# Norm roots spread by two split products, the sample's attention a step earlier, and a last norm with half the sum products

## The chip, the cores and the metric

The kernel runs on one core of a Trainium2 chip. The core has five engines with a queue of instructions each: TensorE (PE: matrix products and transposes, with its weight loads listed apart as PEld), VectorE (DVE), ScalarE (ACT), GpSimd (POOL) and SyncE (SP, which here only issues transfers). Engines run beside one another and wait for each other on semaphores. The metric is the time of one execution on the device in microseconds, lower is better.

## The reference

One layer of a decoder is computed for a prompt of 512 positions and, separately, for 8 samples of 4 new positions with a cache of 128 earlier keys and values. Everything is float32. Each of the two halves of the layer is wrapped in two RMS norms:

```
def _rmsnorm(x, g):
    y = x32 * lax.rsqrt(jnp.mean(x32 * x32, axis=-1, keepdims=True) + EPS) * g
...
h    = rmsnorm(x, norm_mix_pre)
m    = mixer(h)            # input projection, RG-LRU branch, windowed attention, gates, w_out
x    = x + rmsnorm(m, norm_mix_post)
f    = conv_ffn(rmsnorm(x, norm_ffn_pre))   # w_up, causal conv of width 3, gelu, w_down
x    = x + rmsnorm(f, norm_ffn_post)
```

The model width is 1024, the feed-forward width 4096, with 8 query heads and 2 key heads of 128. The sample's attention works on 128 cached and 4 own keys, with a learned sink and a relative bias.

## The kernel before

**Layout.** Activations stand transposed: 8 tiles of 128 channels by 544 columns, 512 positions of the prompt and 32 of the sample. Most stages work on them in two halves of columns, 256 and 288 (HALF) or 272 and 272 (HALF2).

**Products.** All large products are made of split operands: a value is written as the sum of two fp32r tiles, high (H, made on ACT by a copy into fp32r) and low (L, made on DVE by subtracting the high part), and three products HH, LH and HL are added up in PSUM. `wsplit_hi` (L283) and `wsplit_lo` (L290) do this for the weights as they arrive (`raw_*` to `wh_*`, `wl_*`), `wh_e`, `wl_e` are the same for the weights of the feed-forward (L1485, L168).

**Norms.** The columns of a tile are positions, so the root of a norm (one number for each position) has to be repeated over the 128 channels. This is done on PE: DVE multiplies the identity by the roots, which gives a diagonal (`dg`, three tiles of up to 128 columns), and PE multiplies a tile of ones by that diagonal, in plain F32. The result `rep` has each column's root in every partition. There are seven such spreads: two at the start for the norm of `x` (`roots`, L536 to L560, `ps_rep0` with 256 columns and `ps_rep2` with 288), four in `norm_chain` (L1240 and on: `rep_m` and `rep_f` for either half, 272 columns), and one at the end in `finish_b` (`rep_o`, 288 columns). The roots come from sums of squares: `sq_sum` adds squares of the eight channel tiles into `acc` (squares on ACT, sum on DVE), `stats` (L1157) sums over the partitions by products of `acc` with a column of ones (`pst_*`), and `newton_rstd` (L413) takes the root on ACT and refines it in five small DVE instructions.

**The first spread** is issued inside a product of the input projection: `mids` holds functions that run between the products with the weights' high part and those with the low part.

**Last norm.** Before, the squares of the last channel tile went to a tile of their own (`sq7`), and `stats` took three products on `acc` and three on `sq7`. After it, `finish_b` scales each of the eight tiles `ft` (DVE) and adds the residual `x1r` (POOL), two tiles to a step; rows are then turned by PE transposes (`pyo`), copied and stored. Meanwhile PE makes the last products of the first half as rows of tokens (`ptok`).

**The sample's attention** is the generator `sample_attn` (two groups of four samples): loads of the cached keys and values into buffers of the pool `raw` (five buffers, shared with the weights' loads), transposes of the keys on DVE (`kcT`), scores on PE (`pss`), softmax in two parts (`ss`, `st_smp`; DVE and ACT), transposes of the probabilities on PE (`pst`), copies (`spt`), the product with the values (`pso`). Each `yield` hands over to the next step.

**What sets the order.** PE's queue is written in program order. A step is one product of an input tile by a weight tile; `tick` advances a counter by one, and `start_at(t, gen)` starts a generator at step t, `yield n` continues it n steps later (L190 and on). For the mixer the other engines' order is the program's too. From `stats` on (L1157) ACT, DVE and POOL are ordered by a scheduler that looks at dependencies and priorities, so an added instruction can change its neighbours' places. Each engine then runs its queue in that order. Loads wait for their buffer: `raw_wg` (the gates' weights), `raw_in` and the cache blocks use the same five.

Of the kernel before, what the change touches and what calls it, by code (L numbers as in the profile page):

```python
# [11 lines left out]
F32 = mybir.dt.float32  # L12
F32R = mybir.dt.float32r
AF = mybir.ActivationFunctionType
ALU = mybir.AluOpType
AX = mybir.AxisListType

P = 128
# [17 lines left out]
FLAT = SEQ + 7 * DB  # L36
# [37 lines left out]
SAMPLE = (41, 46)  # L74
# [49 lines left out]
def hawk_step(ctx, tc, I, O):  # L124
    nc = tc.nc
    act, dve, pool, pe = nc.scalar, nc.vector, nc.gpsimd, nc.tensor

    keep = ctx.enter_context(tc.tile_pool(name="const", bufs=1))
# [4 lines left out]
    smp = ctx.enter_context(tc.tile_pool(name="small", bufs=4))  # L133
# [12 lines left out]
    def T(name, dt=F32):  # L146
        return tp.tile([P, FLAT + 4], dt, tag="t", name=name)
# [13 lines left out]
    def f32(ap):  # L161
        return ap.bitcast(F32)

    def mm(out, l, r, start, stop):
        pe.matmul(out, l, r, start=start, stop=stop)  # L165

    def sub(out, a, b):
        dve.tensor_tensor(out=out, in0=a, in1=b, op=ALU.subtract)  # L168
# [14 lines left out]
    def start_at(t, gen):  # L183
        serial[0] += 1
        side.append([t, serial[0], gen])
# [29 lines left out]
            tick()  # L215


    ones = keep.tile([P, P], F32, name="ones")
    pool.memset(ones, 1.0)
    ident = keep.tile([P, P], F32, name="ident")  # L220
    make_identity(nc, ident)
    epst = keep.tile([P, 1], F32, name="epst")
    pool.memset(epst, EPS)


    w_in, w_up, w_dn = I["w_in"][0], I["w_up"][0], I["w_down"][0]
# [307 lines left out]
    ps_ohp = []  # L534

    def roots(i0, i1):  # L536
        dg = T(f"dg_{i0}")
        t0 = TOK[i0][0]
        spans = [(TOK[i][0] - t0, TOK[i][1], i) for i in range(i0, i1)]
        n = spans[-1][0] + spans[-1][1]  # L540
        last.append(lambda: xrstd(i0, i1))
        for o, w, i in spans:
            last.append(lambda o=o, w=w, i=i: dve.tensor_scalar(dg[:, o:o + w], ident[:, :w], ss[:, 1, i:i + 1], None,
                                                                ALU.mult))
        yield

        def spread_roots():
            ps = PX(f"ps_rep{i0}")
            mm(ps[:, 0:n], ones, dg[:, 0:n], True, True)
            if not i0:  # L550
                mm(ps[:NH, 256:256 + WIN], relx, ohp, True, True)
                ps_ohp.append(ps)
            act.copy(rep[:, t0:t0 + n], ps[:, 0:n])

        if i0:
            spread_roots()
        else:
            mids.insert(0, spread_roots)
# [318 lines left out]
    def sample_attn(g):  # L877
        kcT = []
        kb = RAW(f"cache_win_k{g}")
        src = I["cache_win_k"][0, 4 * g:4 * g + 4].rearrange("b (e j) k (a d) -> a k j (b e) d", e=4, a=4)  # L880
        for kv in range(NKV):
            for a in range(4):
                nc.sync.dma_start(out=kb[32 * a:32 * a + 32, 512 * kv:512 * kv + 512].rearrange("p (x d) -> p x d", d=32),
                                  in_=src[a, kv])
        vraw = RAW(f"cache_win_v{g}").rearrange("p (b x) -> p b x", b=4)
        nc.sync.dma_start(out=vraw, in_=I["cache_win_v"][0, 4 * g:4 * g + 4].rearrange("b j k d -> j b (k d)"))
        yield 2
        kb4 = kb.rearrange("p (k b x) -> p k b x", k=NKV, b=4)
        for half in range(2):
            kt = S(f"kcT{g}{half}")  # L890
            dve.transpose(kt[:, 0:512].rearrange("p (b k x) -> p k b x", b=2, k=NKV), kb4[:, :, 2 * half:2 * half + 2, :])
            kcT.append(kt)
        yield
        ps = PX(f"pss{g}")
        qg = qs[:, 4 * g:4 * g + 4, :, :].rearrange("p b h t -> p (b h t)")
        mm(ps[:, 2 * WIN:SKEY], qg, kn.rearrange("p k n -> p (k n)"), True, True)
        for b in range(4):
            mm(ps[32 * b:32 * b + 32, 0:2 * WIN], qs[:, 4 * g + b, :, :].rearrange("p h t -> p (h t)"),
               kcT[b // 2][:, (b % 2) * 256:(b % 2) * 256 + 256], True, True)
        yield  # L900
        s = T(f"ss{g}")
        stt(s[:, 0:SKEY], ps[:, 0:SKEY], SCALE, biasS[:, g, :], ALU.mult, ALU.add)
        s3 = s[:, 0:SKEY].rearrange("p (o j) -> p o j", o=1)
        se = softmax_a(s3, 1, sinkr, f"smp{g}")
        yield
        softmax_b(s3, 1, *se)
        yield
        px = PX(f"pst{g}")
        pe.transpose(px[:, 0:P], s[:, 0:P], ident)
        pe.transpose(px[:, P:2 * P], s[:, P:2 * P], ident)  # L910
        pe.transpose(px[:64, 2 * P:3 * P], s[:, 2 * P:SKEY], ident)
        yield
        pt = T(f"spt{g}")
        dve.tensor_copy(pt[:, 0:2 * P], px[:, 0:2 * P])
        dve.tensor_copy(pt[:64, 2 * P:3 * P], px[:64, 2 * P:3 * P])
        yield
        po = PX(f"pso{g}")
        mm(po[:, 0:HD], pt[:64, 2 * P:3 * P], vnt, True, False)
        for kv in range(NKV):
            for b in range(4):  # L920
                mm(po[32 * b:32 * b + 32, 0:HD], pt[:, kv * P + 32 * b:kv * P + 32 * b + 32],
                   vraw[:, b, kv * HD:(kv + 1) * HD], False, kv == NKV - 1)
        yield
        so = T(f"so{g}")[:, 0:HD]
        dve.tensor_copy(so, po[:, 0:HD])
        yield
        px = PX(f"psot{g}")
        pe.transpose(px[:, 0:P], so, ident)
        yield
        ov = px[:, 0:P].rearrange("p (b h t) -> p b h t", b=4, h=NH)  # L930
        parts_ = [[A.t[hd][z][:, SEQ + 16 * g:SEQ + 16 * g + 16].rearrange("p (b t) -> p b t", b=4) for z in range(2)]
                  for hd in range(NH)]
        for hd, (oh, ol) in enumerate(parts_):
            act.activation(oh, ov[:, :, hd, :], AF.Copy)
        yield
        for hd, (oh, ol) in enumerate(parts_):
            sub(ol, ov[:, :, hd, :], f32(oh))
# [124 lines left out]
    start_at(19, sample_rows())  # L1062
    start_at(SAMPLE[0] - 4, scale_qs())
    for g in range(2):
        start_at(SAMPLE[g] - 3, sample_attn(g))
    for c in range(8):
        start_at(GATES[c], gates(c))
        start_at(EXPS[c], lru_exp(c))
# [85 lines left out]
    mixer.close()  # L1154


    def stats(acc, nch, nm, more=None):  # L1157

        ps = PX("pst_" + nm)
        for z in range(nch):  # L1160
            mm(ps[:, z:z + 1], acc[:, z * P:(z + 1) * P], ones[:, 0:1], z == 0, more is None and z == nch - 1)
        for z in range(nch if more is not None else 0):
            mm(ps[:, z:z + 1], more[:, z * P:(z + 1) * P], ones[:, 0:1], False, z == nch - 1)
        st = SM("nst_" + nm, [P, 3, 4], "nst")
        v, r, s_ = (st[:, z, :nch] for z in range(3))
        newton_rstd(r, v, s_, ps[:, :nch])
        return r

    def diag(r, n, nm):
        dg = T("dg_" + nm)  # L1170
        for z in range((n + P - 1) // P):
            w = min(P, n - z * P)
            dve.tensor_scalar(dg[:, z * P:z * P + w], ident[:, :w], r[:, z:z + 1], None, ALU.mult)
        return dg

    def spread(dg, n, nm):

        rep = PX("rep_" + nm)
        mm(rep[:, :n], ones, dg[:, :n], True, True)
        return rep  # L1180

    def sq_sum(acc, src, n, first, nm):
        if first:
            act.activation(acc[:, :n], src, AF.Square)
            if n % P:
                pool.memset(acc[:, n:n + P - n % P], 0.0)
        else:
            sq = T("sq_" + nm)
            act.activation(sq[:, :n], src, AF.Square)
            add(acc[:, :n], acc[:, :n], sq[:, :n])  # L1190
# [538 lines left out]
    x1r = {}  # L1729
# [73 lines left out]
                start_at(now[0] + 3, ffn_states(g0, g1))  # L1803

    yp, ys = O["y_p"][0], O["y_s"].rearrange("b t d -> (b t) d")
    sq7 = {}

    def finish_b(acc):

        lo, hi = HALF[1]  # L1810
        n = hi - lo
        dg = diag(stats(acc, 3, "o1", sq7), n, "o1")
        yield FB[0]
        rep = spread(dg, n, "o1")
        for c in range(8):
            f_ = ft[c][:, lo:hi]
            stt(f_, f_, pv[:, G_FPOST + c:G_FPOST + c + 1], rep[:, :n], ALU.mult, ALU.mult)
            pool.tensor_tensor(out=f_, in0=f_, in1=x1r[c][:, lo:hi], op=ALU.add)
            if c % 2:
                yield 0.5  # L1820

# [10 lines left out]
                between()  # L1832
        return lambda q=nc.sync: q.dma_start(out=dst, in_=o[:nn, :])

    sq7 = T("sq7")
    frow, fgs = {}, {}

    def last_done(c, acc):
        def f(a, ps):
            lo, hi = HALF[a]  # L1840
            n = hi - lo
            f_ = ft[c][:, lo:hi]
            add(f_, f_, ps[:, :n])
            if c < 7:
                sq_sum(acc, f_, n, c == 0, f"ft{a}_{c}")
            else:
                sq_sum(sq7, f_, n, True, "")
        return f

    def turned(i, kk):  # L1850
# [157 lines left out]
```

## Time and profile before

| | |
|---|---|
| median of 3 runs | 977.51 us (977.38 to 977.61) |
| the profiled execution | 977.74 us |
| its span | 976.0 us |
| granted TensorE clock, mean | 0.998 |
| DMA | 147 GB/s mean, 143.07 MB |

A row of the timeline has the start and the length in microseconds, the engine, the line of the program, the operation, output and inputs by the program's names, and where the engine idled before it, for how long and whom it waited for. Rows of the same kind that follow each other directly are put together ("x3"), with the time from the first start to the last end. A matrix product's length is the time from its start until its result is out; products overlap, so what a product costs is read from the distance between starts. An F32 product shows as two records. A row of the list of waits names the waiting and the releasing instruction, then the total wait, how often, and the longest.

### The profile page before, as it was taken

The page shows a single profiled execution, that of the slowest core. Times are in us where ns is not written, and L with a number is a line of the kernel's source. Part 1 is how long each engine was busy: PE and PEld are TensorE (multiplying, and loading weights), DVE is VectorE, ACT ScalarE, POOL GpSimd, SP SyncE. Part 2 cuts the span into 40 slices and gives each one's busy share as a digit, 9 for nine tenths or more (in the row PEclk, how much of TensorE's full clock was granted, in tenths as well). Part 3 has the DMA queues.
Part 4 walks back from the last instruction along what each step waited for, and adds up shares of the span by engine and source line. Part 5 has one row for each costly group of instructions (what it writes and reads, how often), then busy time and mean ns, then how long its engine had stood idle before and what let it go on. Part 6 is the DMA issues. An engine that isn't in the chain of part 4 may idle for free.

```text
span 976.0 us, 20122 instructions
## 1 busy us (share of the span) xinstructions
PE 967.6 (99%) x7668; PEld 959.9 (98%) x7668; DVE 758.6 (78%) x1632; ACT 551.0 (56%) x1344; POOL 168.8 (17%) x288
## 2 busy tenths in 40 slices
PE   9999999999999999999999999999999999999997
PEld 8999999999999999999999999999999999999996
DVE  5777888857858555699967888787888888888875
ACT  6544443467476435556767665655555555556652
POOL 2152000003306331230011111101011101011024
PEclk9999999999999999999999999999999999999999
DMA  7875535632334547136157585858586766768612
GB/s 217 237 239 163 151 88 147 161 93 87 109 113 126 175 121 189 45 122 184 39 114 189 126 191 129 184 137 177 140 179 157 169 156 160 166 140 221 201 30 92
DMA packets 234204, 143.07 MB, mean 147 GB/s; under 512 B 25012, under 2 KB 218940, under 8 KB 234076
## 3 DMA queue, kind: packets, MB, share of 16 engines
q1 hardware_dynamic: 224300, 120.21, 43.9%
q0 software_dynamic: 9696, 19.42, 11.9%
q10 hardware_dynamic: 112, 2.17, 0.6%
q8 instruction: 60, 0.98, 0.4%
q14 instruction: 36, 0.29, 0.1%
HBM read 115.59 MB, written 15.17 MB: 134 GB/s over the span
## 4 chain that ended last, share of the span: by engine, by line
PE 97%; DVE 1%; ACT 1%; DMA 0%; issue 0%; SPq 0%; POOL 0%; ACTq 0%; POOLq 0%
PE pmin L165 20%; PE pmdn L165 19%; PE pux L1536 16%; PE puy L1536 8%; PE pq L1536 7%; PE pmout L165 5%; PE pmlo L165 5%; PE pmao L165 5%; PE puz L1536 4%; PE pg L165 1%; PE pvp L165 1%; PE psc L165 1%; PE ptok L165 1%; DMA pt<-pd 0%; PE ps_warm L165 0%; PE pm_first L165 0%
## 5 line engine op out<-in xcount | busy, mean ns | idle before, releaser
L165 PE MATMUL pmin<-hH,wh_in 128*128 128x256 f32 (+1 forms) x568 | 164.0, 291 | 0.0
L165 PE MATMUL pmin<-hL,wh_in 128*128 128x256 f32 (+1 forms) x568 | 162.5, 288 | 0.0
L165 PE MATMUL pmin<-hH,wl_in 128*128 128x256 f32 (+1 forms) x568 | 159.3, 288 | 0.0
L165 PE MATMUL pmdn<-fH,wh_dn 128*128 128x256 f32 (+1 forms) x448 | 129.3, 289 | 0.0
L165 PE MATMUL pmdn<-fH,wl_dn 128*128 128x256 f32 (+1 forms) x448 | 129.2, 288 | 0.0
L165 PE MATMUL pmdn<-fL,wh_dn 128*128 128x256 f32 (+1 forms) x448 | 129.0, 288 | 0.0
L165 PEld LDWEIGHTS pmin<-hH,wh_in 128*128 128x128 f32 x568 | 107.3, 189 | 1.2 <-issue 1.0
L165 PEld LDWEIGHTS pmin<-hL,wh_in 128*128 128x128 f32 x568 | 107.4, 189 | 0.1
L165 PEld LDWEIGHTS pmin<-hH,wl_in 128*128 128x128 f32 x568 | 104.8, 188 | 0.2 <-issue 0.2
L177 DVE SCALAR_TENSOR_TENSOR uc<-u,fv,uc 128x560 f32<-128x560 f32 x128 | 102.0, 797 | 1.7 <-ACT uc L1567 1.1
L165 PEld LDWEIGHTS pmdn<-fL,wh_dn 128*128 128x128 f32 x448 | 84.4, 188 | 0.0
L165 PEld LDWEIGHTS pmdn<-fH,wl_dn 128*128 128x128 f32 x448 | 84.4, 188 | 0.0
L165 PEld LDWEIGHTS pmdn<-fH,wh_dn 128*128 128x128 f32 x448 | 84.4, 188 | 0.0
L1664 ACT COPY u<-pux 128x272 f32<-128x272 f32 x52 | 20.1, 386 | 84.4 <-PE pux L1536 84.2
L168 DVE TENSOR_TENSOR u<-puy,u 128x240 f32<-128x240 f32 (+2 forms) x78 | 24.6, 343 | 48.8 <-PE puy L1536 32.2
L174 DVE TENSOR_TENSOR ft<-ft,pmdn 128x256 f32<-128x256 f32 (+1 forms) x104 | 45.0, 434 | 15.7 <-PE pmdn L165 15.7
L283 ACT ACTIVATE wh_in<-raw_in 128x512 fp32r<-128x512 f32 x70 | 42.2, 625 | 20.7 <-issue 11.0
L290 DVE TENSOR_TENSOR wl_in<-raw_in,wh_in 128x512 fp32r<-128x512 f32 x70 | 47.8, 694 | 1.0 <-ACT wh_in L283 1.0
L1567 ACT ACTIVATE uc<-u,fv 128x560 f32<-128x560 f32 x64 | 48.2, 755 | 0.0
L779 ACT ACTIVATE s<-s,st 128x256 f32<-128x256 f32 (+1 forms) x32 | 15.2, 475 | 53.8 <-DVE st L776 46.1
L168 DVE TENSOR_TENSOR wl_dn<-raw_dn,wh_dn 128x512 fp32r<-128x512 f32 x56 | 38.3, 685 | 3.8 <-ACT wh_dn L1485 3.8
L1474 POOL DMA_DIRECT2D raw_up_s<-raw_up_s x26 | 22.4, 861 | 95.8 <-DMA raw_up_s<-raw_up__11277 5.4
(761 smaller groups left out, 3388.5 us busy)
## 6 DMA issues: line engine op xcount, KB each, us to landing
raw_in<-in_w_in_dram SPq DMA_DIRECT2D x35, 512.0 KB
raw_dn<-in_w_down_dram SPq DMA_DIRECT2D x56, 256.0 KB
raw_up_s<-in_w_up_dram SPq DMA_DIRECT2D x25, 512.0 KB
raw_up_s<-raw_up_s POOLq DMA_DIRECT2D x26, 256.0 KB, 5.3
raw_ao<-in_w_attn_o_dram SPq DMA_DIRECT2D x8, 512.0 KB
raw_lo<-in_w_lru_o_dram SPq DMA_DIRECT2D x8, 512.0 KB
raw_out<-in_w_out_dram SPq DMA_DIRECT2D x8, 512.0 KB
pd<-pb SPq DMA_DIRECT2D x12, 256.0 KB
```

Source lines behind the costliest of these rows:

```text
L165: pe.matmul(out, l, r, start=start, stop=stop)
L168: dve.tensor_tensor(out=out, in0=a, in1=b, op=ALU.subtract)
L174: dve.tensor_tensor(out=out, in0=a, in1=b, op=ALU.add)
L177: dve.scalar_tensor_tensor(out=out, in0=a, scalar=s_, in1=b, op0=op0, op1=op1)
L283: act.activation(hl[0], raw, AF.Copy)
L290: (eng or dve).tensor_tensor(out=hl[1], in0=raw, in1=f32(hl[0]), op=ALU.subtract)
L779: act.activation(s3[:, j, :], s3[:, j, :], AF.Exp, bias=ng[:, j:j + 1], accum_out=sm[:, j:j + 1])
L1474: pool.dma_start(out=w["p4"], in_=w["p2"], accum_op=ALU.add)
L1536: pe.matmul(ps[:, :HN], w, x, start=start and k == 0 and i == 0, stop=stop and k == 3 and i == 2, skip_group_check=True)
L1567: act.activation(yt[j][:, 0:FLATU], u[:, 0:FLATU], AF.Copy, scale=fv[:, j:j + 1])
L1664: act.copy(e[nm_], z)
```

## The change

Five things change.

1. `ones` becomes an fp32r tile (read as F32 by `stats`). A new `diag` rounds the roots to fp32r (`rh`, a DVE CAST), takes the remainder (`rl`, a DVE subtraction), and makes two diagonals: of `rh` on DVE as before, of `rl` on ACT. `spread_to` then adds two fp32r products in place of one F32 product. All seven spreads use it.
2. `sample_attn` starts one step earlier, and a step is added between its softmax and the transposes, so that the transposes stay where they were and all before them is a step earlier.
3. In the last norm the eighth tile's squares are added into `acc` like the others, and `stats` takes three products.
4. In `finish_b` the residual of odd tiles is added on DVE, that of even tiles on POOL.
5. By these the order of some transfers moves too: the second group's cache block is now loaded ahead of the gates' weights `raw_wg`, in the buffer that `raw_wg` had, and `raw_wg` takes the cache block's later.

```diff
+    onesr = keep.tile([P, P], F32R, name="ones")
+    ones = f32(onesr)
...
+    def diag(r, n, nm):
+        nch = (n + P - 1) // P
+        rs = smp.tile([P, 2, 4], F32R, tag="rs", name="rs_" + nm)
+        rh, rl = (rs[:, z, :nch] for z in range(2))
+        dve.tensor_copy(rh, r)
+        sub(rl, r, f32(rh))
+        wide = 2 * n > FLAT
+        t_ = [T(f"dg{x}_{nm}", F32R) for x in ("hl" if wide else "b")]
+        dh, dl = t_[0][:, 0:n], (t_[1][:, 0:n] if wide else t_[0][:, n:2 * n])
+        for z in range(nch):
+            c = slice(z * P, min(n, z * P + P))
+            w = c.stop - c.start
+            dve.tensor_scalar(dh[:, c], ident[:, :w], f32(rh[:, z:z + 1]), None, ALU.mult)
+            act.activation(dl[:, c], ident[:, :w], AF.Copy, scale=f32(rl[:, z:z + 1]))
+        return dh, dl
+
+    def spread_to(ps, dg):
+        for z in range(2):
+            mm(ps, onesr, dg[z], z == 0, z == 1)
...
-        for o, w, i in spans:
-            last.append(lambda o=o, w=w, i=i: dve.tensor_scalar(dg[:, o:o + w], ident[:, :w], ss[:, 1, i:i + 1], None,
-                                                                ALU.mult))
+        last.append(lambda: dg.extend(diag(ss[:, 1, i0:i1], n, str(i0))))
...
-            mm(ps[:, 0:n], ones, dg[:, 0:n], True, True)
+            spread_to(ps[:, 0:n], dg)
...
         softmax_b(s3, 1, *se)
-        yield
+        yield 2
...
-        start_at(SAMPLE[g] - 3, sample_attn(g))
+        start_at(SAMPLE[g] - 4, sample_attn(g))
...
-        mm(rep[:, :n], ones, dg[:, :n], True, True)
+        spread_to(rep[:, :n], dg)
...
-        dg = diag(stats(acc, 3, "o1", sq7), n, "o1")
+        dg = diag(stats(acc, 3, "o1"), n, "o1")
...
-            pool.tensor_tensor(out=f_, in0=f_, in1=x1r[c][:, lo:hi], op=ALU.add)
+            (dve if c % 2 else pool).tensor_tensor(out=f_, in0=f_, in1=x1r[c][:, lo:hi], op=ALU.add)
...
-            if c < 7:
-                sq_sum(acc, f_, n, c == 0, f"ft{a}_{c}")
-            else:
-                sq_sum(sq7, f_, n, True, "")
+            sq_sum(acc, f_, n, c == 0, f"ft{a}_{c}")
```

How this moves instructions is shown at three places. A row has the line, the operation, and output and inputs.

ACT at the first spread, before: `ss` is the root of the first two blocks of positions, `wh0_in_8` and `wh1_in_8` the high parts of a weight tile that PE needs next, `rep` the copy of the spread roots.

```order
L435 ACTIVATE jk0_1_313,ss_169<-x0_1_107 128x512
L418 ACTIVATE ss_169<-ss_169,epst_95 128x2
L283 ACTIVATE wh0_in_8_353<-raw_in_8_114 128x512
L283 ACTIVATE wh1_in_8_356<-raw_in_8_114 128x512
L553 COPY rep_257<-ps_rep0_378 128x256
```

The same stretch of ACT's queue now:

```order
L457 ACTIVATE jk0_1_313,ss_169<-x0_1_107 128x512
L440 ACTIVATE ss_169<-ss_169,epst_95 128x2
L240 ACTIVATE dgb_0_328<-ident_90,rs_0_325 128x128 x2
L305 ACTIVATE wh0_in_8_358<-raw_in_8_114 128x512
L305 ACTIVATE wh1_in_8_361<-raw_in_8_114 128x512
L572 COPY rep_257<-ps_rep0_383 128x256
```

The two low diagonals, which read the remainder `rs_0`, now stand between the root and the copies of the weights.

DVE at the spread `rep_m` of the first half, before: `nst_m0` are the roots, `dg_m0` their diagonals, `wl_e` the low part of a weight tile whose high part ACT makes.

```order
L177 SCALAR_TENSOR_TENSOR nst_m0_5641<-nst_m0_5641 128x3 x2
L1173 TENSOR_SCALAR dg_m0_5661<-ident_90,nst_m0_5641 128x128 x2
L1173 TENSOR_SCALAR dg_m0_5661<-ident_90,nst_m0_5641 128x16
L168 TENSOR_TENSOR wl_e_0_1_5877<-raw_up_0__5781,wh_e_0_1_5876 128x512
L177 SCALAR_TENSOR_TENSOR mt0_5289<-mt0_5289,pv_141,rep_m0_5681 128x272
```

And the same place of DVE's queue now, with `rs_m0` for the rounded roots and their remainder:

```order
L177 SCALAR_TENSOR_TENSOR nst_m0_5655<-nst_m0_5655 128x3 x2
L231 CAST rs_m0_5675<-nst_m0_5655 128x3
L168 TENSOR_TENSOR wl_e_0_1_5904<-raw_up_0__5802,wh_e_0_1_5903 128x512
L168 TENSOR_TENSOR rs_m0_5675<-nst_m0_5655,rs_m0_5675 128x3
L239 TENSOR_SCALAR dgb_m0_5678<-ident_90,rs_m0_5675 128x128 x2
L239 TENSOR_SCALAR dgb_m0_5678<-ident_90,rs_m0_5675 128x16
L177 SCALAR_TENSOR_TENSOR mt0_5303<-mt0_5303,pv_141,rep_m0_5701 128x272
```

The weight's low part now stands between the rounding and the remainder, ahead of the diagonals. At the other three spreads of `norm_chain` the CAST, the remainder and the diagonals stand together where the diagonals were.

DVE in the second group of the sample's attention, before: `s3_3` is a softmax of the prompt, `wl1_in_5` a weight's low part, `spt0` the copies of the first group's turned probabilities, `kcT10` and `kcT11` the second group's turned keys.

```order
L787 TENSOR_SCALAR s3_3_2623<-s3_3_2623,st_3_3_2625 128x256 x2
L290 TENSOR_TENSOR wl1_in_5_2674<-raw_in_5_2378,wh1_in_5_2673 128x512
L171 TENSOR_TENSOR xr4_2676<-pmin_4_1_2648,rep_257 128x256
L171 TENSOR_TENSOR xr4_2676<-pmin_4_1_2648,rep_257 128x8x4
L168 TENSOR_TENSOR tL3_1_2732<-pt3_1_2556,tH3_1_2731 128x512
L821 STREAM_TRANSPOSE pb3_3_2735<-s3_3_2623 128x512
L914 COPY spt0_2739<-pst0_2692 128x256
L915 COPY spt0_2739<-pst0_2692 64x128
L891 STREAM_TRANSPOSE kcT10_2742<-cache_win_k1_2636 128x2x2x128
L891 STREAM_TRANSPOSE kcT11_2744<-cache_win_k1_2636 128x2x2x128
```

The same stretch now:

```order
L806 TENSOR_SCALAR s3_3_2651<-s3_3_2651,st_3_3_2653 128x256 x2
L910 STREAM_TRANSPOSE kcT10_2710<-cache_win_k1_2598 128x2x2x128
L910 STREAM_TRANSPOSE kcT11_2712<-cache_win_k1_2598 128x2x2x128
L312 TENSOR_TENSOR wl1_in_5_2688<-raw_in_5_2392,wh1_in_5_2687 128x512
L171 TENSOR_TENSOR xr4_2690<-pmin_4_1_2662,rep_257 128x256
L171 TENSOR_TENSOR xr4_2690<-pmin_4_1_2662,rep_257 128x8x4
```

The transposes moved ahead of the weight's low part. On PE the second group's scores `pss1` moved from behind `pso0` to ahead of the products of `pmin_33_1` (the second half of the step before).

More of the change, by code (lines that the diff above doesn't have):

```diff
@@ L215, in flush @@
             tick()
-    ones = keep.tile([P, P], F32, name="ones")
+    onesr = keep.tile([P, P], F32R, name="ones")
+    ones = f32(onesr)
     pool.memset(ones, 1.0)
@@ L536, in roots @@
     def roots(i0, i1):
-        dg = T(f"dg_{i0}")
+        dg = []
         t0 = TOK[i0][0]
-        spans = [(TOK[i][0] - t0, TOK[i][1], i) for i in range(i0, i1)]
-        n = spans[-1][0] + spans[-1][1]
+        n = TOK[i1 - 1][0] + TOK[i1 - 1][1] - t0
         last.append(lambda: xrstd(i0, i1))
-        for o, w, i in spans:
-            last.append(lambda o=o, w=w, i=i: dve.tensor_scalar(dg[:, o:o + w], ident[:, :w], ss[:, 1, i:i + 1], None,
-                                                                ALU.mult))
+        last.append(lambda: dg.extend(diag(ss[:, 1, i0:i1], n, str(i0))))
         yield
@@ L1154, in hawk_step, with stats @@
     mixer.close()
-    def stats(acc, nch, nm, more=None):
+    def stats(acc, nch, nm):
         ps = PX("pst_" + nm)
         for z in range(nch):
-            mm(ps[:, z:z + 1], acc[:, z * P:(z + 1) * P], ones[:, 0:1], z == 0, more is None and z == nch - 1)
-        for z in range(nch if more is not None else 0):
-            mm(ps[:, z:z + 1], more[:, z * P:(z + 1) * P], ones[:, 0:1], False, z == nch - 1)
+            mm(ps[:, z:z + 1], acc[:, z * P:(z + 1) * P], ones[:, 0:1], z == 0, z == nch - 1)
         st = SM("nst_" + nm, [P, 3, 4], "nst")
@@ L1167, in stats @@
         return r
[L1169 to L1174, printed above, removed]
     def spread(dg, n, nm):
         rep = PX("rep_" + nm)
-        mm(rep[:, :n], ones, dg[:, :n], True, True)
+        spread_to(rep[:, :n], dg)
         return rep
@@ L1805, in hawk_step @@
     yp, ys = O["y_p"][0], O["y_s"].rearrange("b t d -> (b t) d")
-    sq7 = {}
     def finish_b(acc):
@@ L1833, in rows_t @@
         return lambda q=nc.sync: q.dma_start(out=dst, in_=o[:nn, :])
-    sq7 = T("sq7")
     frow, fgs = {}, {}
```

## The prediction

> **What bounds the kernel now.** I read the page first, its span, the busy time and the chain that ended last, and then the list of everything TensorE (PE) waited for.
>
> ```profile
> span 976.0 us, 20122 instructions
> ...
> PE 967.6 (99%) x7668; PEld 959.9 (98%) x7668; DVE 758.6 (78%) x1632; ACT 551.0 (56%) x1344; POOL 168.8 (17%) x288
> ...
> PE 97%; DVE 1%; ACT 1%; DMA 0%; issue 0%; SPq 0%; POOL 0%; ACTq 0%; POOLq 0%
> ```
>
> ```profile
> PE ps_warm L165 <- POOL ones L219: 1.0, 1, 1.0
> PE pst L909 <- DVE ss L787: 0.7, 1, 0.7
> PE pm_first L165 <- DVE wh_in L285: 0.6, 1, 0.6
> ```
>
> PE is busy for 967.6 of 976.0 us and in its whole program it waits three times, 2.3 us together. So the rule for every part below is simple: a microsecond of PE work removed, or of PE waiting added, moves the end by as much, and work of the other engines counts only where PE then waits for it. The reader should therefore look, at each place, at the slack between an engine's row and the PE row that needs it; with so few waits in the list most slacks are positive but short.
>
> **What the seven products save.** A spread multiplies a diagonal by ones.
>
> ```profile
> 399.63 0.62 PE L165 MATMUL rep_m<-dg_m,ones 128*128 128x272 f32 x2
> ...
> 400.21 0.29 PE L165 MATMUL pmout<-mL,wh_out 128*128 128x272 f32 x1
> 400.34 0.29 PE L165 MATMUL pmout<-mH,wl_out 128*128 128x272 f32 x1
> ```
>
> Products of split (fp32r) operands with 272 columns follow each other every 0.13 us (400.21 to 400.34). From 399.63 to 400.21 stand the F32 product and one such product, so the F32 one holds PE for 0.58 − 0.125 = 0.455. Two split products take 0.25: 0.205 saved. By columns that is 0.19 for the first spread (256) and 0.22 for the two with 288, in all 0.19 + 2 × 0.22 + 4 × 0.205 = 1.45 us.
>
> [...]
>
> **What the split costs: before every spread a longer chain.** The new `diag` puts a CAST and a subtraction of a 128x3 column ahead of the diagonals on DVE and gives ACT as many diagonal tiles again. Neither operation of this size into these types is in the trace; neighbours of that size follow at about 0.2 us, so I take 0.4 for both (bounds 0.3 and 0.5). The seven places follow.
>
> First spread (A):
>
> ```profile
> 13.42 0.30 ACT L418 ACTIVATE ss<-ss,epst 128x2 f32<-128x2 f32 x1 [0.49 <-DVE ss L174]
> 13.62 1.14 ACT L283 ACTIVATE wh_in<-raw_in 128x512 fp32r<-128x512 f32 x2
> ...
> 14.14 0.36 DVE L177 SCALAR_TENSOR_TENSOR ss<-ss 128x2 f32<-128x2 f32 x2
> ...
> 14.60 0.48 DVE L543 TENSOR_SCALAR dg<-ident,ss 128x128 f32<-128x128 f32 x2
> ...
> 14.91 0.19 PEld L165 LDWEIGHTS pmin<-hH,wh_in 128*128 128x128 f32 x1
> ...
> 36.11 0.30 ACT L710 COPY klast<-ks 128x128 f32<-128x128 f32 x1
> ```
>
> Before, ACT goes from the root at 13.42 straight to the two `wh_in` copies, and PE loads the first of them at 14.91. Now the two low diagonals stand between (the order in the section on the change). They need the remainder, which DVE has at 14.50 + 0.4 = 14.90; two ACT copies of 128x128 (0.30, the second 0.2 later) end near 15.45; the first `wh_in` can begin about 0.1 before that, as at 13.62, and takes 0.62, so it is there at 15.97. PE stands still for 15.97 − 14.91 = **1.07**; the spread behind it (dg ready near 15.4, needed 16.9 before) then saves 0.19: **+0.88**. Bounds: −0.19 if ACT were somehow past, +1.0 if each of the small steps is 0.05 longer.
>
> [...]
>
> Second spread (B), and the first one of the norm behind `w_out` (C):
>
> ```profile
> 33.19 0.64 DVE L543 TENSOR_SCALAR dg<-ident,ss 128x128 f32<-128x128 f32 x3
> ...
> 33.97 0.72 PE L165 MATMUL ps_rep<-dg,ones 128*128 128x288 f32 x2
> ```
>
> ```profile
> 398.86 0.69 DVE L168 TENSOR_TENSOR wl_e<-raw_up__5781,wh_e 128x512 fp32r<-128x512 f32 x1
> ```
>
> B has no slack: the diagonals end at 33.83 and PE starts at 33.97. With 0.4 more PE waits 0.4 and saves 0.22: **+0.18** (0 to +0.3). At C the diagonals stood ahead of `wl_e`; now only the CAST does, and the subtraction and diagonals are behind it. `wl_e` waits for its own ACT copy, so it still ends at 399.55. The subtraction adds 0.1 to 0.2, three diagonals 0.62 (the row at 412.57 below), so they end at 400.28 and PE starts at 400.33 and not 399.63: 0.70 waited, 0.2 saved, **+0.50** (−0.2 to +0.7).
>
> The other three of the two middle norms (D, E, F):
>
> ```profile
> 412.57 0.62 DVE L1173 TENSOR_SCALAR dg_f<-ident,nst_f 128x128 f32<-128x128 f32 x3
> ...
> 413.44 0.43 ACT L1189 ACTIVATE sq_wo<-mt 128x272 f32<-128x272 f32 x1
> ...
> 414.32 0.62 PE L165 MATMUL rep_f<-dg_f,ones 128*128 128x272 f32 x2
> ...
> 422.98 0.63 DVE L1173 TENSOR_SCALAR dg_m<-ident,nst_m 128x128 f32<-128x128 f32 x3
> ...
> 424.73 0.62 PE L165 MATMUL rep_m<-dg_m,ones 128*128 128x272 f32 x2
> ...
> 440.44 0.62 DVE L1173 TENSOR_SCALAR dg_f<-ident,nst_f 128x128 f32<-128x128 f32 x3
> ...
> 441.21 0.63 PE L165 MATMUL rep_f<-dg_f,ones 128*128 128x272 f32 x2
> ```
>
> D and E have slacks of 1.1 on DVE, which cover 0.4. At D the low diagonals come behind `sq_wo` on ACT and end near 414.45, and the second product needs them at 414.45: covered, barely. So **−0.20** each (0 if ACT is 0.2 later). F has 0.15 of slack: 441.46 + 0.05 against 441.21, 0.30 waited, 0.2 saved, **+0.10** (−0.2 to +0.3, because ACT's next weight copy now stands behind the diagonals and delays what follows by some 0.6).
>
> **The last norm (G)** loses three of six sum products, but its PE work now waits for one more DVE addition.
>
> ```profile
> 947.87 0.46 DVE L174 TENSOR_TENSOR acc<-acc,sq_ft 128x288 f32<-128x288 f32 x1 [0.51 <-ACT sq_ft L1189]
> ...
> 948.73 0.44 ACT L1184 ACTIVATE sq<-ft 128x288 f32<-128x288 f32 x1 [0.89 <-DVE ft L174]
> ...
> 949.08 0.73 PE L165 MATMUL pst_o<-ones,acc 128*128 128x1 f32 x6
> 949.67 0.81 PE L165 MATMUL pst_o<-ones,sq 128*128 128x1 f32 x6
> 950.34 0.36 PE L165 MATMUL pmdn<-fH,wh_dn 128*128 128x256 f32 x1
> ...
> 951.68 0.63 DVE L1173 TENSOR_SCALAR dg_o<-ident,nst_o 128x128 f32<-128x128 f32 x3
> ...
> 953.27 0.65 PE L165 MATMUL rep_o<-dg_o,ones 128*128 128x288 f32 x2
> ```
>
> Before, the first three products on `acc` ran while ACT still made the squares of the last column. Now they wait: squares until 949.17, addition 0.46, so PE starts near 949.75 and not 949.08, about 0.70 with its weight load; the three products that are gone held it for 950.34 − 949.67 = 0.67. That is a swap, **+0.03** (−0.67 to +0.15). The chain behind ends about 0.5 later than 952.31 and PE asks at 953.27, so the spread keeps its 0.22: together **−0.19**.
>
> **The residuals (H)** move four additions from POOL to DVE.
>
> ```profile
> 954.56 4.63 POOL L1818 TENSOR_TENSOR ft<-ft,x1r 128x288 f32<-128x288 f32 x6 [11.21 <-DVE ft L177]
> ...
> 962.55 1.03 PE L1829 MATMUL pyo<-ident,ft 128*128 128x128 f32 x8
> ```
>
> POOL takes 0.77 for each and is through before PE turns the rows at 962.55; PE has its token products to do in between, and they are the cover. **0**; if the cover failed on DVE, the four additions (at most 4 × 0.46, as at 947.87) would have to fit into 8 us.
>
> **The sample's attention (S).** Starting it a step earlier lets the softmax end a step before the transposes, so the 0.67 wait on `ss` in the second fence goes. But the second group's cache transposes now have to be ready earlier.
>
> ```profile
> 171.73 0.68 DVE L290 TENSOR_TENSOR wl_in<-raw_in,wh_in 128x512 fp32r<-128x512 f32 x1
> ...
> 172.55 0.30 PE L165 MATMUL pmin<-hH,wh_in 128*128 128x288 f32 x1
> ...
> 176.10 1.27 DVE L891 STREAM_TRANSPOSE kcT<-cache_win_k 128x512 f32<-128x512 f32 x2
> ```
>
> The two `kcT` transposes (1.27) now stand ahead of that `wl_in`, and the second group's score products ahead of the product at 172.55, which the vanished wait brings to 171.88. On DVE I count the pieces moved earlier as equal to those gone from here, with 0.3 gained from an idle stretch, so the transposes run from 171.4 to 172.7, while PE needs the second about 172.15: 0.55 waited. Taken with 0.02 for small shifts: −0.67 + 0.57 = **−0.10** (−0.67 to +0.4).
>
> **Sum**: 0.88 + 0.18 + 0.50 − 0.20 − 0.20 + 0.10 − 0.19 + 0 − 0.10 = **+0.97 us**. The profiled execution took 977.74 us, 1.74 of it around its span; it would take 978.7. It lies 0.23 above the median of the runs shown, 977.51, so the median comes to **978.5**. A measurement of this kernel tells about 0.2%, that is 1.95 us, from no change: the forecast lies inside that.
>
> **Rivals.**
> 1. *The waits don't come, the savings do.* For it: seven products shorter is certain, and slack of several of these chains is off by only tenths. Against it: at A the engine's order alone makes the wait. If A, C, F and S's new wait are all absent: −1.45 for the spreads, −0.67 for `ss`, and 0.03 + 0.40 for G and B, −1.7, thus 975.8; with G's wait absent too −2.4, 975.1. Chance 0.13, and half of this case passes the 1.95.
> 2. *Slower by a late gate weight.* Place: ACT around 180.
>
> ```profile
> 172.88 2.63 SPq L829 DMA_DIRECT2D pt<-pd  x4
> ...
> 179.13 0.63 ACT L832 ACTIVATE tH<-pt 128x512 fp32r<-128x512 f32 x1 [1.80 <-DMA pt<-pd]
> ...
> 184.64 0.28 PE L165 MATMUL pvp<-tH,vH 128*128 128x256 f32 x1
> ```
>
> `raw_wg` is now loaded into the buffer that the second cache block leaves, so SP's queue stands until the transposes are done (172.7), and the `pt` loads stand behind it; on ACT the `wh_wg` copy stands ahead of `tH`. A load of this queue landed 3.6 us after its last issue (172.88 + 2.63 to 179.13). With that `raw_wg` is there by 177.5 and `tH` near 181, 3 us before PE asks at 184.64. Behind the load stand four steps of 0.6 to 0.7 (`wh_wg`, `aH`, `tH` and DVE's remainder of it), 2.6 in all, so it may take about 8.5 us; beyond that PE waits, and at 10.5 us it loses 2, and the time is 980.5. Nothing in the list of waits speaks for so slow a load. Chance 0.07.
> 3. *The same mechanism, every small step dearer* (A +1.0, B +0.3, C +0.7, D and E 0, F +0.3, G −0.07, S +0.4): +2.6, 980.1. Chance 0.08.
> 4. *It does not do what it says*: were the split products held as long as the F32 one each, every spread would lose 0.45 and not save 0.2, +4.5, 982.0. The many split products at 0.125 speak against it. Chance 0.02.
>
> **How the numbers follow.** The forecast, 977.4 to 979.4, has 0.70. The range reaches down into half of rival 1 and up to rival 3: 976.4 to 980.1. Faster by over 0.2% takes half of rival 1 and a little of the rest, 0.08; slower takes rivals 2 to 4 in most of their parts, 0.14; within, 0.78.
>
> **What would show it.** In the profile after: PE's list of waits should have a new first row, `pmin` on ACT `wh_in` with about 1.1; `rep_m` on DVE with 0.7; smaller ones for `ps_rep`, `rep_f` and `pst_o` (0.3 to 0.7), `pss` on `kcT` with 0.5, and none for `pst` on `ss`. The seven spreads should show products 0.13 apart. Wrong would be: no wait at `wh_in`, which takes 1.1 from the sum; waits on `raw_wg` or `tH`; or a span away by over 2 us with the waits as named.

## The result, and the profile after

The changed kernel took 980.27 us (median of 7 runs, 980.06 to 981.57) against 977.51 us before (7 runs, 977.31 to 977.61): a ratio of 1.0030, 95% interval 1.0018 to 1.0042. It is slower by 2.8 us. The forecast was 978.5, with a range to 980.1.

The page of the changed kernel, its span and busy times, in the same form as before:

```profile
span 978.2 us, 20145 instructions
...
PE 967.8 (99%) x7662; PEld 958.8 (98%) x7662; DVE 763.4 (78%) x1651; ACT 556.4 (57%) x1364; POOL 166.6 (17%) x283
```

PE's busy time did not fall although its products became cheaper: a product behind a wait is recorded as 0.37 to 0.39 us long (`ps_rep` at 35.23, `pmin` at 16.12, below) and not 0.28 to 0.30, so part of the waiting counts as busy. The list of PE's waits in the changed kernel (waiting and releasing instruction, total, times, longest):

```profile
PE pmin L165 <- ACT wh_in L305: 1.0, 1, 1.0
PE ps_warm L165 <- POOL ones L220: 1.0, 1, 1.0
PE pm_first L165 <- DVE wh_in L307: 0.8, 1, 0.8
PE pst_o L165 <- DVE acc L174: 0.5, 1, 0.5
PE rep_m L165 <- DVE dgb_m L239: 0.4, 1, 0.4
PE pst_f L165 <- DVE accx L174: 0.3, 1, 0.3
PE ps_rep L165 <- DVE rq L593: 0.2, 1, 0.2
```

The three waits of before became seven. `pst` on `ss` is gone, as forecast; `wh_in`, `pst_o`, `rep_m`, `ps_rep` came, as forecast; `pst_f` was not foreseen. Two that were forecast are missing from the list, `rep_f` and `pss` on `kcT`, and yet both are in the timeline: it shows the weight loads of `pss` waiting for `kcT` for 0.17 and 0.45, and `rep_f` below. The list is not the whole: these two waits of weight loads are not in it, nor is the one between the two products of `rep_f` (416.05 to 416.68, below). The sum is better read from the same PE row in both timelines. Since PE does nearly the same products in both, the difference of two starts is the delay gathered so far:

| PE row, and the part between it and the row above | before | after | delay |
|---|---|---|---|
| `pmin` with the first weights' high part, last row | 13.96 | 13.87 | −0.09 |
| `ps_rep` on `ohp`, behind the first spread (A) | 17.45 | 18.45 | +1.00 |
| `pmin` behind the second spread (B) | 34.66 | 35.91 | +1.25 |
| `pmin` ahead of the first sample group's transposes | 168.43 | 169.69 | +1.26 |
| `pmin` behind both groups' scores (S) | 180.74 | 181.81 | +1.07 |
| `pmout` behind the first `rep_m` (C) | 400.21 | 401.95 | +1.74 |
| `pmout` behind the first `rep_f` (D) | 414.90 | 416.81 | +1.91 |
| `pq` behind the second `rep_m` (E) | 425.45 | 427.16 | +1.71 |
| `pst_f` of the second half | 437.43 | 439.37 | +1.94 |
| `pq` behind the second `rep_f` (F) | 441.80 | 444.08 | +2.28 |
| `pq` on the second half of `b22` | 448.96 | 451.44 | +2.48 |
| `pmdn` behind the last sums (G) | 950.54 | 953.11 | +2.57 |
| `ptok` behind the last spread | 954.22 | 956.55 | +2.33 |
| last `pyo` | 968.47 | 970.79 | +2.32 |

So 2.3 us of the 2.8 are delay of PE's stream. Of the rest, 0.3 lies around the span of the two profiled executions (980.27 − 978.2 against 977.74 − 976.0), and the profiled execution of before was itself 0.2 above its median. The delay arises at the places that the forecast named and at two behind them that its sum put at nothing (`pst_f`, and the products on `b22`, a tile made from the result of spread F). A, C, D and F are dearer than it said by 0.2 to 0.4 each.

What a spread looks like now, first where there is slack (E), then where there is little (D), in the timeline of the changed kernel:

```profile
425.17 0.62 DVE L239 TENSOR_SCALAR dgb_m<-ident,rs_m 128x128 fp32r<-128x128 f32 x3
425.28 0.90 ACT L240 ACTIVATE dgb_m<-ident,rs_m 128x128 fp32r<-128x128 f32 x3 [1.30 <-DVE rs_m L168]
426.66 0.41 PE L165 MATMUL rep_m<-dgb_m,ones 128*128 128x272 f32 x2
426.91 0.29 PE L1546 MATMUL pq<-b21H,wh_e 128*128 128x272 f32 x1
...
414.58 0.62 DVE L239 TENSOR_SCALAR dgb_f<-ident,rs_f 128x128 fp32r<-128x128 f32 x3
415.52 0.88 ACT L240 ACTIVATE dgb_f<-ident,rs_f 128x128 fp32r<-128x128 f32 x3
416.05 0.79 PE L165 MATMUL rep_f<-dgb_f,ones 128*128 128x272 f32 x2
416.68 0.29 PE L165 MATMUL pmout<-mH,wh_out 128*128 128x272 f32 x1
```

The rows at B and C in the same timeline:

```profile
34.58 0.91 ACT L240 ACTIVATE dgl<-ident,rs 128x128 fp32r<-128x128 f32 x3 [1.24 <-DVE rs L168]
35.23 0.37 PE L165 MATMUL ps_rep<-dgh,ones 128*128 128x288 f32 x1 [0.23 <-DVE rq L593]
35.54 0.40 PE L165 MATMUL ps_rep<-dgl,ones 128*128 128x288 f32 x1
35.77 0.30 PE L165 MATMUL pmin<-hH,wh_in 128*128 128x288 f32 x1
...
400.65 0.89 ACT L240 ACTIVATE dgb_m<-ident,rs_m 128x128 fp32r<-128x128 f32 x3 [0.83 <-DVE rs_m L168]
401.20 0.78 PE L165 MATMUL rep_m<-dgb_m,ones 128*128 128x272 f32 x2 [0.42 <-DVE dgb_m L239]
401.82 0.29 PE L165 MATMUL pmout<-mH,wh_out 128*128 128x272 f32 x1
```

The rows at A, then those behind E and at F:

```profile
14.86 0.69 ACT L240 ACTIVATE dgb<-ident,rs 128x128 fp32r<-128x128 f32 x2 [1.22 <-DVE rs L168]
15.46 1.14 ACT L305 ACTIVATE wh_in<-raw_in 128x512 fp32r<-128x512 f32 x2
16.12 0.39 PE L165 MATMUL pmin<-hH,wh_in 128*128 128x256 f32 x1 [1.03 <-ACT wh_in L305]
16.34 0.28 PE L165 MATMUL pmin<-hL,wh_in 128*128 128x256 f32 x1
...
426.73 0.69 DVE L168 TENSOR_TENSOR wl_e<-raw_up__5808,wh_e 128x512 fp32r<-128x512 f32 x1 [0.94 <-ACT wh_e L1495]
...
439.37 0.83 PE L165 MATMUL pst_f<-ones,accx 128*128 128x1 f32 x6 [0.27 <-DVE accx L174]
...
442.77 0.89 ACT L240 ACTIVATE dgb_f<-ident,rs_f 128x128 fp32r<-128x128 f32 x3 [1.48 <-DVE rs_f L168]
443.33 0.78 PE L165 MATMUL rep_f<-dgb_f,ones 128*128 128x272 f32 x2
443.95 0.30 PE L1546 MATMUL pq<-b11H,wh_e 128*128 128x272 f32 x1
```

At E the two products hold PE for 426.91 − 426.66 = 0.25, as forecast. At D it is 416.68 − 416.05 = 0.63: the high diagonals were ready at 415.20, but the low ones on ACT only at 415.52 + 0.88 = 416.40, and the second product waits for them. No row of the list of waits shows this; the distance of the rows does. C and F are held for 0.62 in the same way, on top of their wait for the first product, and B for 0.54.

### The profile page after: what moved, and what is told of

It reads as the page before. It is cut to its first block, busy times and chain, and to the rows that moved or that the text cites. A ratio compares the mean times of both kernels' runs of the same rounds, so it can differ in the third digit from the quotient of the medians.

```text
span 978.2 us, 20145 instructions
## 1 busy us (share of the span) xinstructions
PE 967.8 (99%) x7662; PEld 958.8 (98%) x7662; DVE 763.4 (78%) x1651; ACT 556.4 (57%) x1364; POOL 166.6 (17%) x283
## 4 chain that ended last, share of the span: by engine, by line
PE 92%; DVE 4%; ACT 2%; issue 0%; POOL 0%; DVEq 0%; ACTq 0%; POOLq 0%
PE pmin L165 21%; PE pmdn L165 16%; PE pux L1546 16%; PE puy L1546 8%; PE pq L1546 6%; PE pmlo L165 5%; PE pmao L165 5%; PE pmout L165 5%; PE puz L1546 4%; PE pg L165 1%; PE psc L165 1%; PE pvp L165 1%; PE ptok L165 1%; DVE wl_e L168 1%; DVE wl_dl L168 0%
```

## The experiments

Each kernel was timed in turn with the kernel before on one chip; ratios below are against that. Delays are read from PE rows as in the table above, for a single spread from the rows directly ahead of it and behind it. Against the kernel before, the row at 13.96 lies between 0.5 earlier and 0.3 later in these profiles, ahead of the first spread, so delays count from that row on.

**1 to 4: which part, which engine, which order.** The first two kernels split the change:

```diff
-        yield 2
+        yield
...
-        start_at(SAMPLE[g] - 4, sample_attn(g))
+        start_at(SAMPLE[g] - 3, sample_attn(g))
...
-        dg = diag(stats(acc, 3, "o1"), n, "o1")
+        dg = diag(stats(acc, 3, "o1", sq7), n, "o1")
...
-            (dve if c % 2 else pool).tensor_tensor(out=f_, in0=f_, in1=x1r[c][:, lo:hi], op=ALU.add)
+            pool.tensor_tensor(out=f_, in0=f_, in1=x1r[c][:, lo:hi], op=ALU.add)
```

for the spreads alone, and for the rest alone

```diff
-            act.activation(dl[:, c], ident[:, :w], AF.Copy, scale=f32(rl[:, z:z + 1]))
...
-        for z in range(2):
-            mm(ps, onesr, dg[z], z == 0, z == 1)
+        mm(ps, ones, dg[0], True, True)
```

> Only the spreads are split; the sample's attention, the last norm's sums and the residuals stay as before. Theory 1 (the diagonals' longer chain on DVE and ACT, with the low diagonals on ACT dearer than was put): nearly all of the loss is here, about +2.5 us on the span against the kernel before, at the same seven places as in the changed kernel (first spread +1.1, second +0.24, the first of the middle norms +0.75, and so on). Rival (the moved sample steps, the transfers or the last norm carry it): at most +1.0, as the prediction's terms for the spreads gave.

> The spreads stay one F32 product; the earlier sample, the halved sums of the last norm and the residuals on two engines are in. Theory 1: within 0.3 us of the kernel before, about -0.15 from the sample and +0.1 from the last norm. Rival (the rest carries the loss): +1 to +2 us.

Measured: the spreads alone 980.66 us against 977.81, ratio 1.0027 (1.0016 to 1.0038); the rest alone 977.94, ratio 1.0002 (0.9993 to 1.0011). The loss is in the spreads. At A, B, C, D, E, `pst_f` and F the spreads alone show the delays of the changed kernel within 0.05 us.

The third moves the low diagonals to DVE, in a loop of their own behind the high ones; the fourth moves only those of the first spread (kept in `lows`), behind the next weights' copies on ACT:

```diff
-            act.activation(dl[:, c], ident[:, :w], AF.Copy, scale=f32(rl[:, z:z + 1]))
+            dve.tensor_scalar(dl[:, c], ident[:, :w], f32(rl[:, z:z + 1]), None, ALU.mult)
```

```diff
         yield
+        for f in lows:
+            f()
+        lows.clear()
 
         def spread_roots():
```

> The changed kernel with all low diagonals made on DVE behind the high ones. Theory 1: the wait for the weights' copies at the first spread is gone (-1.3 us), at the tight spreads the second product waits 0.1 to 0.2 longer because DVE makes both in turn, the weights' copy behind the last spread of the middle norms is no longer late (-0.2): about -1.0 us against the changed kernel, so +1.7 against the kernel before. Rival (the CAST and the subtraction make the waits, whoever makes the diagonals): the waits of PE stay, the time stays within 0.3 us of the changed kernel.

> The changed kernel with the two low diagonals of the first spread written behind the next weight tile's two copies on ACT; nothing else moves. If the order on ACT alone makes the wait at the first spread, it goes wholly: the first spread turns from +1.1 to -0.2, thus -1.3 us against the changed kernel. Rival (the copies are late for another reason, such as their buffer or the load): the wait at wh_in stays near 1.0.

Measured against 977.81: low diagonals on DVE 979.70 us (ratio 1.0018, 1.0009 to 1.0027), a loss of 1.9; behind the copies 979.16 (1.0016, 1.0007 to 1.0025), a loss of 1.35. The changed kernel lost 2.76, so by the medians they are better than it by 0.9 and 1.4; the intervals overlap with its own, and the places in PE's rows are the firmer sign. In both, the wait of 1.0 at `wh_in` is gone. ACT and PE of the fourth kernel at the first spread:

```profile
13.04 0.30 ACT L450 ACTIVATE ss<-ss,epst 128x2 f32<-128x2 f32 x1 [0.43 <-DVE ss L174]
13.24 1.14 ACT L315 ACTIVATE wh_in<-raw_in 128x512 fp32r<-128x512 f32 x2
14.56 0.70 ACT L242 ACTIVATE dgb<-ident,rs 128x128 fp32r<-128x128 f32 x2 [0.18 <-DVE rs L168]
...
16.54 0.40 PE L165 MATMUL ps_rep<-dgb,ones 128*128 128x256 f32 x2
```

The copies follow the root at once as before, the diagonals end at 15.26 and PE takes them at 16.54: more than a microsecond of slack, and this spread now gains 0.2. The order on ACT alone made that wait.

The third kernel shows why DVE is no cure elsewhere. DVE and PE at the first `rep_f`:

```profile
414.54 0.44 DVE L174 TENSOR_TENSOR acc<-acc,sq_wo 128x272 f32<-128x272 f32 x1 [0.44 <-ACT sq_wo L1205]
414.90 0.62 DVE L244 TENSOR_SCALAR dgb_f<-ident,rs_f 128x128 fp32r<-128x128 f32 x3
...
414.94 0.29 PE L165 MATMUL rep_f<-dgb_f,ones 128*128 128x272 f32 x1
415.57 0.39 PE L165 MATMUL rep_f<-dgb_f,ones 128*128 128x272 f32 x1 [0.34 <-DVE dgb_f L244]
```

Here the second product waits openly, 0.63 behind the first and not 0.13. Made on either engine, the low half comes last: B cost 0.40, C 0.89, D 0.40 and F 0.46 here, each 0.1 to 0.2 more than in the changed kernel. The delays at `b22` behind F and at `pst_f` are gone, now that ACT has no diagonals ahead of its weight copies.

**5: the low half left out.** This kernel leaves out the remainder, the low diagonals and the second product, so its roots are rounded to fp32r.

```diff
         dve.tensor_copy(rh, r)
-        sub(rl, r, f32(rh))
...
-            act.activation(dl[:, c], ident[:, :w], AF.Copy, scale=f32(rl[:, z:z + 1]))
-        return dh, dl
+        return (dh,)
```

> The changed kernel with only the rounded roots: the remainder, the low diagonals and the second product of each spread are left out, so the roots are rounded to fp32r. It shows what the CAST alone costs. Theory 1 (the low half on ACT makes most of the waits): first spread -0.3 against the kernel before, second about -0.1, the first middle one +0.3 (its diagonals still stand behind the weight's low part, 0.57 waited, 0.33 saved), the next two -0.33, the last middle one -0.2, the last -0.36: about -1.1 us in PE's stream against the kernel before, 3.4 under the changed kernel. Rival (the CAST and the longer chain on DVE carry it): above the kernel before.

Measured: 976.59 us, ratio 0.9988 (0.9979 to 0.9997). PE at the two spreads that matter:

```profile
399.18 0.39 PE L165 MATMUL rep_m<-dgb_m,ones 128*128 128x272 f32 x1 [0.35 <-DVE dgb_m L236]
399.42 0.29 PE L165 MATMUL pmout<-mH,wh_out 128*128 128x272 f32 x1
...
413.64 0.29 PE L165 MATMUL rep_f<-dgb_f,ones 128*128 128x272 f32 x1
413.77 0.29 PE L165 MATMUL pmout<-mH,wh_out 128*128 128x272 f32 x1
```

D holds PE for 0.13 with no wait. Spread by spread the gains against the kernel before are 0.32 (A), 0.16 (B), −0.29 (C, whose diagonals stand behind the weight's low part here too), 0.34 (D), 0.33 (E), 0.13 (F) and 0.37 (last), each within 0.1 of what was expected, and `pst_f` and `b22` cost nothing. So the CAST with its place in DVE's queue costs little, but for C. Each against the kernel before timed beside it, this kernel gains 1.3 us where the changed one loses 2.8, so the low half (remainder, diagonals and products together) costs about 4 us; the spans of the two profiles say the same, 978.2 − 974.2. Its seven products are only about 0.9 of it (7 × 0.13): the rest is waiting for it and behind it.

**6 to 8: the other parts, one by one.**

Against the kernel before, the sample alone, the last norm alone and the residuals alone are:

```diff
-        start_at(SAMPLE[g] - 3, sample_attn(g))
+        start_at(SAMPLE[g] - 4, sample_attn(g))
...
-        yield
+        yield 2
```

```diff
-            if c < 7:
-                sq_sum(acc, f_, n, c == 0, f"ft{a}_{c}")
-            else:
-                sq_sum(sq7, f_, n, True, "")
+            sq_sum(acc, f_, n, c == 0, f"ft{a}_{c}")
```

```diff
-            pool.tensor_tensor(out=f_, in0=f_, in1=x1r[c][:, lo:hi], op=ALU.add)
+            (dve if c % 2 else pool).tensor_tensor(out=f_, in0=f_, in1=x1r[c][:, lo:hi], op=ALU.add)
```

> Only the sample's attention starts a step earlier; spreads, last norm and residuals as before. By the trace of the changed kernel the wait on ss goes (-0.86 with what follows it) and the second group's scores wait for the turned keys (+0.70): -0.15 us in PE's stream. The time around the span was 1.8 us in the kernel before and in the spreads alone, and about 2.05 in the three other kernels: if the moved transfers cause it, it is 2.05 here and the time comes out 0.1 above before; if not, 1.8 and 0.15 below.

> Only the last norm's eighth tile is added into the common sum, with three sum products in place of six. PE waits 0.5 for the addition and saves 0.67: within 0.1 us of before in PE's stream. Around the span: 1.8 if the last norm has nothing to do with it, 2.05 if it has.

> Only the residuals of odd tiles move from POOL to DVE. Prediction's term: 0 in PE's stream. Around the span: 1.8 if the residuals have nothing to do with it, 2.05 if POOL's or DVE's shorter or longer queue at the end makes it.

Measured against 977.74: 978.04 (ratio 1.0001, 0.9993 to 1.0010), 978.21 (1.0006, 0.9997 to 1.0015) and 977.97 (1.0004, 0.9995 to 1.0012): none can be told from before. In PE's stream the sample alone gives −0.15 and the last norm +0.10, as expected. The time around the span has a median of 1.99 us with the sample alone and 1.80 and 1.78 with the others, against 1.77 for the kernel before in the same runs. It is 2.0 in the changed kernel too. So the earlier sample adds about 0.2 us outside the span; how it does so is not settled.

**9 to 11: versions with the split only where there is slack.** The mix splits the first spread (low diagonals behind the copies), the second `rep_m` (low ones on DVE) and the last; the other four stay in F32, the last norm and residuals as before, the sample a step earlier. The other two start only the first group of the sample earlier, once alone and once in the mix:

```diff
-        yield 2
+        yield 1 if g else 2
...
-        start_at(SAMPLE[g] - 4, sample_attn(g))
+        start_at(SAMPLE[g] - (3 if g else 4), sample_attn(g))
```

> The sample a step earlier; split spreads only where the slack is long enough: the first (its low diagonals behind the weights' copies), the second half's rep_m (low diagonals on DVE) and the last; the other four spreads in F32; last norm and residuals as before. Theory 1: first spread -0.2, second half's rep_m -0.2, last spread -0.22, sample -0.15, no new wait: -0.75 us in PE's stream against the kernel before. Rival (a spread's saving is taken back by the chain behind it, as at the wait of pst_f on accx in the changed kernel): -0.4 to -0.55, with a wait of about 0.2 at pst_f.

> Only the first group of the sample's attention starts a step earlier, the second stays where it was; all else as before. If the second group's turned keys make the wait that takes back the gain, that wait (0.70) is gone and PE's stream ends 0.86 us earlier than before. Around the span: 1.8 if the second cache block's place ahead of the gates' weights makes the longer time around it, 2.05 if the first group's earlier loads do. Rival (the wait is only shifted to another place of the first group): -0.15 as with both groups.

> The mix of before with only the first group of the sample early. Three spreads -0.2 each and -0.86: -1.45 us in PE's stream against the kernel before, and, if the time around the span stays 1.8, the median -1.4 (ratio 0.9985). Rival (the gains are taken back behind): no faster than the mix, -0.5.

Measured: the mix 977.28 us against 977.74, ratio 0.9993 (0.9985 to 1.0002); the first group alone 977.62 against 977.92, 0.9998 (0.9989 to 1.0007); the mix with it 976.92 against 977.92, 0.9992 (0.9983 to 1.0001). In the mix each of the three spreads saves 0.19 to 0.25 and there is no new wait at `pst_f`: E's saving stays once ACT has no diagonals there. The two versions of the mix have the best medians of those that compute the whole, but their intervals reach 1. The time around the span is 1.92 with the first group alone (1.79 before, in the same runs), so the first group's earlier start is enough to lengthen it.

The first group alone gains less than expected, 0.3 by the medians and not 0.86, and the mix with it 1.0 and not 1.4. PE's list of waits there:

```profile
PE pm_first L165 <- DVE wh_in L297: 1.0, 1, 1.0
PE ps_warm L165 <- POOL ones L219: 1.0, 1, 1.0
PE pux L1538 <- DVE wl_s_p L168: 0.8, 1, 0.8
PE pso L165 <- DVE spt L924: 0.2, 1, 0.2
```

The wait for the second group's keys is gone, but 0.2 of the gain is lost at `pso`, and much more at 888 us, at a weight's low part. DVE there, before and in this kernel:

```profile
886.05 0.69 DVE L174 TENSOR_TENSOR p<-raw_up_s,raw_up__12416 128x512 f32<-128x512 f32 x1 [1.64 <-DMA raw_up_s<-in_w_up_dram]
```

```profile
886.65 0.69 DVE L174 TENSOR_TENSOR p<-raw_up_s,raw_up__12416 128x512 f32<-128x512 f32 x1 [2.98 <-DMA raw_up_s<-in_w_up_dram]
```

DVE waits for a load, and although this kernel's PE was 0.8 us ahead, the load landed 0.6 later. PE lost 1.1 us there in this profile, 0.7 with the residuals alone, 0.4 in the spreads alone, in the low diagonals on DVE and in the mix with the first group, 0.1 in the mix, and nothing in the changed kernel's. This place has only about 0.2 us of slack before: against PE, DVE's row is 1.3 later here and 0.9 later with the residuals alone, and PE lost 0.2 less than that each time. So it takes from earlier gains what the load's landing decides.

## Why the prediction was wrong

The direction of the sum was right, its size was not: +0.97 forecast, +2.76 measured, 0.2 beyond the range.

- **The rule** (PE's time moves the end) held: 2.3 us of PE's delay went to the end.
- **What a product saves** was right: the split spreads hold PE for 0.25 at 272 columns where nothing waits (E, the mix), and the last one saved 0.22 to 0.25.
- **The step that failed is when the low diagonals are ready.** The prediction put "two ACT copies of 128x128 (0.30, the second 0.2 later)", from a COPY, and so about 0.7 for three, and used them only at A and D. They took 0.69 for two and 0.88 to 0.91 for three. At B, C and F its sum has no term for them at all, and at D it said "covered, barely": they ended at 416.40, when the second product would have started at 416.18. From the rows, these spreads hold PE for 0.62 to 0.63 at C, D and F and for 0.54 at B, where 0.25 and 0.27 were forecast: **0.37 three times and 0.27**. A part of this is the wait itself, a part that the product behind a wait is followed later: by 0.22 at A (16.12 to 16.34) and 0.24 at C of experiment 5, where no low half is waited for, and not by 0.13.
- **Place by place**, from the differences in the table, the sum was missed by 0.37 at D, 0.24 at F, 0.23 at `pst_f`, 0.21 at A, 0.20 at `b22`, 0.17 at C, 0.07 at B and 0.06 at G, and by −0.09 at S. Without the low half (experiment 5) A, B, D, F, `pst_f` and `b22` cost nothing, and only C still does.
- **A second term was off the other way, and that is luck.** The CAST and the subtraction were put at 0.4 (bounds 0.3 and 0.5). From the start of the CAST to the start of the diagonals it is 0.28 to 0.29 (34.17 to 34.46 at B, 414.30 to 414.58 at D); at C, where only the subtraction counts, the diagonals start 0.07 behind it (400.46 to 400.53) and not 0.1 to 0.2. So PE waited 0.1 less than forecast for the first product at B, C and F, which hid part of the wait for the second: B came near its forecast by two errors.
- **A** was right in mechanism and place: PE waited 1.0 and the wait went with the order on ACT (experiment 4). It cost 1.09 and not 0.88, by the dearer diagonals and the slower first product behind the wait.
- **C** waited for the first product somewhat less than put (0.6 and not 0.7), and was held 0.37 longer than forecast from there on.
- **E** saved 0.2 as forecast, and gave it back at `pst_f` (0.23): the chain on DVE, POOL and ACT between the spread and the next sums stood behind DVE's `wl_e`, which waited 0.94 for ACT's copy, and that copy stood behind ACT's diagonals.
- **F**'s tail, put at zero in the sum with a bound of 0.3 for all, cost 0.20 at `b22`, in the same way: DVE's `wl_e` at 444.22 waited 0.94 for ACT's copy, which began at 443.57 behind the diagonals.
- **G, H and S** came within 0.1 of +0.03, 0 and −0.10 in PE's stream. S has 0.2 outside the span that no step of the prediction had.
- **The rivals**: "the waits don't come" fell; a late gate weight cost nothing (`tH` began at 183.02 and not 179.13, and PE's delay did not grow there); "every small step dearer" (980.1) was nearest in time, though it raised the price of the chain ahead of the first product, which came cheaper than put, and it was the second product that waited.

## What to carry to other kernels

When one product is replaced by two, the second one's operand has its own time of readiness, and it must be checked against PE at every place, not only where its engine has other work: here the saving was 0.19 to 0.25 us at a spread where nothing waits, and a second operand that came late cost 0.27 to 0.37 at four of seven. Split only where the slack of the later operand exceeds its whole chain, and put it behind whatever PE needs sooner on that engine. Read delays from the same row in both timelines: a list of waits can lack those between products of one group, as the 0.63 at D.

## What was not expected of the hardware

- Three ACTIVATE of up to 128x128 with a scale for each partition took 0.88 to 0.91 us on ACT, three such products on DVE 0.62 to 0.63.
- The product behind a wait of PE was followed 0.22 to 0.24 us later (A, and C of experiment 5), where its neighbours follow each other every 0.12 to 0.13.
- The time around the span differs between kernels that do the same work: its median is about 1.8 us in the kernel before and in the three others that leave the sample in place, 1.9 to 2.1 in the nine that start it earlier. The cause is open.
- The landing of one weight load near 886 us, set against PE's rows, was 0.9 us later than before with the residuals alone and 1.3 with the first group alone, and PE lost 0.7 and 1.1 us there. Each kernel has one profile, so whether the kernel or the single execution makes it is open.
